# Weight splits on one engine, phase ends reordered by an issue-order constraint, and a recurrence with its state scans between the gate branches

## The chip, the cores and the metric

The kernel runs on one core of one Trainium2 chip, and all work of a forward pass is in this one launch. The metric is device time in microseconds (us) of one execution. Three runs of the kernel before took 1542.88, 1546.4 and 1547.67 us; the median is 1546.4.

A core has five engines that the text names: TensorE (PE in the rows, with its weight loads apart as PEld), VectorE (DVE), ScalarE (ACT), GpSimd (POOL) and SyncE (SP), which here issues every weight transfer. Each engine works through its own queue in order, and engines wait for each other through semaphores.

## The reference, cut to what matters

The input is 256 tokens of width 1024, in fp32, with 256 context tokens. Two blocks follow each other. The first is two layers that mix attention, pooling and a gated linear recurrence; the change leaves most of it alone. The second block is what this text is about:

```
for layer in range(2):
    h = rmsnorm_2(x, norm_mix_pre[layer])
    m = attention_mixer(h, ...) if layer == 0 else recurrent_mixer(h, ...)
    x = x + rmsnorm_2(m, norm_mix_post[layer])
    h = rmsnorm_2(x, norm_ffn_pre[layer])
    f = (silu(h @ w_gate) * (h @ w_up)) @ w_down
    x = x + rmsnorm_2(f, norm_ffn_post[layer])
```

The recurrent mixer, which is the part with changed arithmetic order:

```
gate, xr = split(h @ w_in, 2);  gate = gelu_tanh(gate)
xc = causal depthwise conv of width 4 over xr, + conv_b
r = sigmoid(xc_blocks @ w_a + b_a);  i = sigmoid(xc_blocks @ w_i + b_i)
log_a = -8 * r * softplus(-lam);  a = exp(log_a)
u = sqrt(-expm1(2 * log_a)) * (i * xc)
hs[t] = a[t] * hs[t-1] + u[t]
out = (hs * gate) @ w_out
```

## The kernel before

Every fp32 matmul is made of three products of fp32r halves: each operand is split into a high part (a copy in the narrower type) and a low part (the difference). `mm3` issues high x high, high x low and low x high for each slice of 128 (L395 to L397), called a product below when one such matmul is meant.

A weight tile is 128 x 1024 numbers (512 KB). `W` has SyncE fetch it to a buffer `wr` (L361), ScalarE writes the high part `wh` (L377), and the low part `wl` is a subtraction (L379):

```
        nlo[0] += 1
        S.activation(ch.h, r, AF.Copy)
        eng = G if lopool[0] and nlo[0] % lopool[0] == 0 else V
        eng.tensor_tensor(ch.l, r, ch.h.bitcast(F32), op=OP.subtract)
```

VectorE does the subtraction, but where `lopool` is set every sixth (in `load`) or every third (in the recurrence) goes to GpSimd. `wr`, `wh` and `wl` have three buffers each; `load` fetches a phase's weights ahead, and its tiles 2 to 6 go to five further held buffers (`HW`).

The 256 tokens are two tiles of 128. The phases named below, with their times in the profiled execution: the last projection of the first block (`wout`, 884 to 913 us), the attention's value projection and attention (to 1023), its output projection `ao` (1023 to 1050), the first feed-forward `ffn0` (to 1243), the recurrence (1243 to 1327) with its output projection `ro` (to 1346), and the second feed-forward `ffn1` (1349 to 1533). An output projection (`out_proj`) runs, for each tile, four groups of 24 products (`as2`), one for each 256 columns. A group's result stands in one of three PSUM buffers `mm`. `out_evac` takes it out: ScalarE squares it with a sum (L429) and VectorE multiplies it by a gain (L579). When a tile is done, `residual` scales and adds it (GpSimd's L419 for the inverse root, VectorE's L574, twice 512 columns), and `prenorm` makes the next phase's input: two Squares on ScalarE (L429), L553 on VectorE, L419 on GpSimd, two scalings on VectorE (L557), eight transposes on TensorE (L560), and the split of the transposed tile into `xnah` on ScalarE (L385) and `xnal` on VectorE (L386). Tile 0's chain runs while TensorE does tile 1's products. The next phase's first products need tile 0's `xnah`.

In the recurrence, `conv(i)` is 24 products and three taps on VectorE (L1458); `gates(n)` is 16 products on raw fp32 operands (L1466) for two channel groups, then Tanh, a scaling on VectorE (L1474), Exp and Tanh; `states` is one Sqrt over four channel groups (L1485) with a table load on ScalarE before and after, multiplications on GpSimd (L1487) and scans on VectorE (L1488). `gelu(4)` to `gelu(7)` are 24 products each, a Square (L1493), a VectorE step (L1494), a Tanh (L1495) and a second VectorE step (L1496) that reads the PSUM buffer for the last time. The result is multiplied by the state (L1505) and split for `ro` into `xnbh` on ScalarE (L388) and `xnbl` on VectorE (L389). Where no constraint is written, the order of instructions on an engine is set by a scheduler when the kernel is built, from data dependences, buffers and priorities.

## Time and profile before

| profiled execution | value |
|---|---|
| its own time | 1548.55 us |
| span of the trace | 1546.7 us |
| mean granted TensorE clock | 0.988 of full speed |
| TensorE busy | 1485.1 us, 96% of the span |
| VectorE busy | 955.3 us, 62% |
| ScalarE busy | 757.8 us, 49% |
| GpSimd busy | 248.5 us, 16% |
| weight transfers of 512 KB | 398, median 3.6 us from issue to landing |

The page gives for each engine the time in which it worked; a share of 96% means that TensorE stood still for some 60 us in all. Where those are, and what ended each of them, is read from the waits and the timeline. The granted clock is TensorE's clock as a share of full speed; in the rows below it has two levels, 1.00 (2.4 GHz) and 0.50 (1.2 GHz), and a value between is a mean over a stretch. TensorE works in the order of its queue, and a matmul of 256 columns is shown with 0.28 us though the next starts 0.12 us later, since they are pipelined.

### The profile page before, as it was taken

What the parts mean: (1) busy time and instruction counts of PE and PEld (TensorE: products, weight loads), DVE (VectorE), ACT (ScalarE), POOL (GpSimd) and SP (SyncE); (2) the same over time, 40 slices, a digit from 0 to 9 for tenths busy, and PEclk for the clock granted to TensorE, in tenths of its full rate; (3) what the DMA queues carried; (4) which work ended last, traced back from release to release, by engine and by line L of the source; (5) the groups of instructions that cost most, each with busy time, mean ns of one, the idle gap of its engine ahead of it and who ended that gap; (6) DMA issues with size and microseconds to landing.
All of it is one profiled execution on the core that took longest, in us unless ns stands there. A gap on an engine that the chain in (4) does not pass through costs nothing.

```text
span 1546.7 us, 25517 instructions
## 1 busy us (share of the span) xinstructions
PE 1485.1 (96%) x10206; PEld 1277.8 (83%) x10206; DVE 955.3 (62%) x1530; ACT 757.8 (49%) x1267; POOL 248.5 (16%) x225
## 2 busy tenths in 40 slices
PE   6999999999999999999999989999999997899998
PEld 3766668787877789878989989879999886899986
DVE  5555545866444567766786654866665567756654
ACT  4444344463423356656565454554444458534443
POOL 0101103624200000113442020321000024100000
PEclk8999999999999999999999999999999998899999
DMA  8433322223334465326446563324566654435564
GB/s 341 126 101 131 123 91 82 65 68 95 96 109 151 135 207 160 116 76 207 158 149 193 170 224 124 123 95 157 185 187 185 214 191 148 151 116 186 180 191 134
DMA packets 65639, 229.79 MB, mean 149 GB/s; under 512 B 7280, under 2 KB 7920, under 8 KB 65392
## 3 DMA queue, kind: packets, MB, share of 16 engines
q1 hardware_dynamic: 65520, 228.16, 46.0%
q8 instruction: 80, 1.31, 0.3%
q14 instruction: 39, 0.32, 0.1%
HBM read 227.09 MB, written 1.05 MB: 147 GB/s over the span
## 4 chain that ended last, share of the span: by engine, by line
PE 81%; DVE 6%; DMA 4%; issue 3%; ACT 3%; POOL 2%; SPq 0%; POOLq 0%; DVEq 0%; ACTq 0%
PE mm L395 22%; PE mm L397 22%; PE mm L396 22%; DMA wr<-in_w_dram 3%; PE at L735 2%; DVE wl L379 2%; PE aux L768 2%; ACT wh L377 2%; PE at L755 1%; PE at L859 1%; PE mm L466 1%; POOL wl L379 1%; POOL E L915 1%; POOL qp L895 1%; PE aux L466 0%
## 5 line engine op out<-in xcount | busy, mean ns | idle before, releaser
L379 DVE TENSOR_TENSOR wl<-wr,wh 128x1024 fp32r<-128x1024 f32 x339 | 425.5, 1257 | 340.2 <-ACT wh L377 338.5
L377 ACT ACTIVATE wh<-wr 128x1024 fp32r<-128x1024 f32 x352 | 370.6, 1055 | 426.3 <-PE mm L396 149.7
L395 PE MATMUL mm<-xnah,wh 128*128 128x256 f32 (+1 forms) x1192 | 368.9, 310 | 11.5 <-DVE rt L1496 10.3
L397 PE MATMUL mm<-xnah,wl 128*128 128x256 f32 (+1 forms) x1192 | 363.2, 305 | 4.0 <-DVE wl L379 4.0
L396 PE MATMUL mm<-xnal,wh 128*128 128x256 f32 (+1 forms) x1192 | 361.7, 304 | 0.0
L395 PEld LDWEIGHTS mm<-xnah,wh 128*128 128x128 f32 x1192 | 226.9, 190 | 27.4 <-DVE rt L1496 10.5
L397 PEld LDWEIGHTS mm<-xnah,wl 128*128 128x128 f32 x1192 | 226.8, 190 | 17.3 <-DVE wl L379 5.4
L396 PEld LDWEIGHTS mm<-xnal,wh 128*128 128x128 f32 x1192 | 227.1, 191 | 9.7 <-issue 1.4
L419 POOL TENSOR_TENSOR sm<-sm,minus_half 128x1 f32<-128x1 f32 (+3 forms) x34 | 26.3, 776 | 695.3 <-DVE sm L567 357.6
L397 PE MATMUL mm<-xnbh,wl 128*128 128x512 f32 (+1 forms) x392 | 136.7, 349 | 0.0
L395 PE MATMUL mm<-xnbh,wh 128*128 128x512 f32 (+1 forms) x392 | 135.0, 345 | 0.0
L396 PE MATMUL mm<-xnbl,wh 128*128 128x512 f32 (+1 forms) x392 | 134.8, 344 | 0.0
L395 PE MATMUL mm<-wh,xnah 128*128 128x256 f32 x288 | 83.4, 291 | 6.4 <-ACT xnah L385 6.1
L397 PEld LDWEIGHTS mm<-xnbh,wl 128*128 128x128 f32 x392 | 73.9, 188 | 11.8 <-issue 3.1
L395 PEld LDWEIGHTS mm<-xnbh,wh 128*128 128x128 f32 x392 | 74.0, 189 | 11.2 <-issue 2.9
L397 PE MATMUL mm<-wh,xnal 128*128 128x256 f32 x288 | 82.2, 289 | 0.8 <-DVE xnal L386 0.6
L396 PE MATMUL mm<-wl,xnah 128*128 128x256 f32 x288 | 82.7, 289 | 0.0
L396 PEld LDWEIGHTS mm<-xnbl,wh 128*128 128x128 f32 x392 | 73.9, 188 | 10.1 <-issue 1.2
L396 PE MATMUL mm<-wl,hh 128*128 128x512 f32 x176 | 69.1, 393 | 0.2 <-DVE wl L379 0.2
L397 PE MATMUL mm<-wh,hl 128*128 128x512 f32 x176 | 68.8, 391 | 0.0
L395 PE MATMUL mm<-yh,wh 128*128 128x512 f32 (+1 forms) x192 | 64.9, 338 | 0.0
L396 PE MATMUL mm<-yl,wh 128*128 128x512 f32 (+1 forms) x192 | 64.9, 338 | 0.0
(373 smaller groups left out, 2821.3 us busy)
## 6 DMA issues: line engine op xcount, KB each, us to landing
wr<-in_w_dram SPq DMA_DIRECT2D x398, 512.0 KB, 3.6
wr<-in_w_dram SPq DMA_DIRECT2D x18, 256.0 KB, 3.2
row<-in_rows_dram SPq DMA_DIRECT2D x8, 512.0 KB, 4.9
xt<-in_xin_dram SPq DMA_DIRECT2D x4, 512.0 KB, 5.7
scr<-in_rows_dram SPq DMA_DIRECT2D x8, 256.0 KB, 4.6
xr<-in_xin_dram SPq DMA_DIRECT2D x2, 512.0 KB, 4.6
xc<-in_xin_dram SPq DMA_DIRECT2D x2, 512.0 KB, 5.3
toep<-in_toep_dram SPq DMA_DIRECT2D x1, 1024.0 KB, 7.2
```

The costliest lines, as they stand in the source:

```text
L377: S.activation(ch.h, r, AF.Copy)
L379: eng.tensor_tensor(ch.l, r, ch.h.bitcast(F32), op=OP.subtract)
L395: T.matmul(dst, lh, rh, start=first and i == 0, stop=False)
L396: T.matmul(dst, lh, rl, start=False, stop=False)
L397: T.matmul(dst, ll, rh, start=False, stop=last and i == n - 1)
L419: G.tensor_tensor(y, m, minus_half[:, :n], op=OP.pow)
L466: T.matmul(p[32 * j:32 * j + 32, c0:c0 + 256], sc[:, k * 32:k * 32 + 32], r[:, j, :], start=half == 0, stop=half == 1, tile_position=(0, 3 ...
L735: T.matmul(pa[:, :n], qxs[pr, j][:, c0 + qt * P:c0 + qt * P + P], kxs[pr, j][:, :n], start=True, stop=True)
L755: T.transpose(pa[:, k * 256 + qt * P:k * 256 + qt * P + P], r[qt][:, (2 * k2 + k) * P:(2 * k2 + k + 1) * P], ident)
L768: T.matmul(py[64 * j:64 * j + 64, c0:c0 + 256], v[:, k, h * 64:h * 64 + 64], pTs[j][k // 2][:, k % 2, :], start=k == 0, stop=k == nk - 1, ...
L859: T.matmul(pa[c * s:c * s + s, t * 2 * s:(t + 1) * 2 * s], k_[:, i:i + s], q_[:, :, j:j + s], start=True, stop=True, tile_position=(0, c * s))
L895: (V, G)[j].tensor_tensor(b[r, j, :], gq[r], e[r], op=OP.mult)
```

## The change

First, every weight's low part is computed on VectorE: the choice by `lopool` is gone, and the 13 subtractions that GpSimd did are VectorE's.

Second, `behind(ins)` fixes an issue order within an engine: what is built inside it is queued behind `ins` if both are on the same engine; nothing waits for it on another engine. It is used three times. `load` queues the splits of its third and later weights behind tile 0's last Square on ScalarE and behind tile 0's last scaling (L557) on VectorE, where a `prenorm` of tile 0 came just before. The last group of tile 1 in `out_proj` (columns 768 to 1023) queues its second 12 products behind tile 0's transposes. The last six products (512 columns) of a feed-forward's tile 1 do the same.

Third, in the recurrence: the scaling L1474 is folded into the scale and bias operands of Exp and Tanh, which drops eight VectorE instructions and adds one small one early in the kernel; `states(0, 4)` stands before `gates(3)`; the four products with the gate of channel groups 0 to 3 come before the last gate matmuls' activations, the four remaining gelu branches write into `gl` in place, `states(4, 8)` is written behind the sixth of them, and the four last products with the gate stand at the end. The buffers `t` go from six to four. `gate_half` is defined and not called.

```diff
-    nlo = [0]
     ahead = [0]
-    lopool = [0]
...
         t = pl.tile([P, width], F32, tag="wr", name=nm("wr"), bufs=bufs)
...
         ch.l = tl[:, :nkt * n].rearrange("p (k c) -> p k c", k=nkt)
-        nlo[0] += 1
         S.activation(ch.h, r, AF.Copy)
-        eng = G if lopool[0] and nlo[0] % lopool[0] == 0 else V
-        eng.tensor_tensor(ch.l, r, ch.h.bitcast(F32), op=OP.subtract)
+        V.tensor_tensor(ch.l, r, ch.h.bitcast(F32), op=OP.subtract)
         return ch
...
     def split(o, sl, src, scale=None):
...
-        S.activation(out, src, AF.Square, scale=float(D) ** -0.5, accum_out=acc)
+        return S.activation(out, src, AF.Square, scale=float(D) ** -0.5, accum_out=acc)
...
         t = scratch()
...
         for c in range(2):
-            sq(b[:, c * 512:c * 512 + 512], xt[:, c * 512:c * 512 + 512], ss[:, c:c + 1])
+            q = sq(b[:, c * 512:c * 512 + 512], xt[:, c * 512:c * 512 + 512], ss[:, c:c + 1])
         s1 = sm(1)
...
             sl = slice(k4 * 512, k4 * 512 + 512)
-            V.scalar_tensor_tensor(b[:, sl], xt[:, sl], y, g[:, sl], op0=OP.mult, op1=OP.mult)
+            m = V.scalar_tensor_tensor(b[:, sl], xt[:, sl], y, g[:, sl], op0=OP.mult, op1=OP.mult)
             p = atps()
             for k in range(4):
-                T.transpose(p[:, k * P:(k + 1) * P], b[:, (4 * k4 + k) * P:(4 * k4 + k + 1) * P], ident)
+                tr = T.transpose(p[:, k * P:(k + 1) * P], b[:, (4 * k4 + k) * P:(4 * k4 + k + 1) * P], ident)
             split(xn, (ALL, slice(4 * k4, 4 * k4 + 4), slice(t * P, t * P + P)), p.rearrange("p (k t) -> p k t", k=4))
+        if t == 0:
+            normed[:] = [q, m]
+        return tr
...
     def residual(xt, op, ssp, n):
...
+    normed = [None, None]
     hold = []
...
-        was = lopool[0]
-        lopool[0] = 6
-        r = [HW(k) if 2 <= i < 2 + NHOLD else W(k) for i, k in enumerate(keys)]
-        lopool[0] = was
+        q, m = normed
+        normed[:] = [None, None]
+        r = []
+        for i, k in enumerate(keys):
+            with behind(q if i >= 2 else None), behind(m if i >= 2 else None):
+                r.append(HW(k) if 2 <= i < 2 + NHOLD else W(k))
         return r
...
         chs = load([keyf(cb, hf) for cb in range(4) for hf in range(2)])
+        tr = None
         for i, (tk, xt, gb) in enumerate(tiles):
...
             for cb in range(4):
-                out_evac(as2(chs[2 * cb:2 * cb + 2], a, slice(tk, tk + P)), 256, ops[i], cb * 256, ssp[:, cb:cb + 1], gb)
+                d = as2(chs[2 * cb:2 * cb + 2], a, slice(tk, tk + P), tr if cb == 3 else None)
+                out_evac(d, 256, ops[i], cb * 256, ssp[:, cb:cb + 1], gb)
             with tc.high_priority(offset=600):
                 residual(xt, ops[i], ssp, 4)
-                after(i)
+                tr = after(i)
...
     def trunk_core(l, M, modfill):
-        lopool[0] = 0
         with ExitStack() as st:
...
             pb, m1 = M.poolb(mp), M.merge(1, lambda: M.yp, True)
...
                 drain(fill)
-        lopool[0] = 0
...
     md0, md1, M0, M1 = Obj(), Obj(), Obj(), Obj()
...
     e, s, s2, acc = sm(8), sm(8), sm(8), sm(8)
-    nsp = const.tile([P, 8], F32, name="nsp")
+    nsp = const.tile([P, 16], F32, name="nsp")
     hb = const.tile([P, 16], F32, name="hb")
...
     S.activation(e, e, AF.Exp, scale=-1.0)
...
     V.scalar_tensor_tensor(acc, acc, 2.0, s, op0=OP.mult, op1=OP.add)
-    V.tensor_scalar(nsp, acc, -4.0, None, op0=OP.mult)
+    for i, f in enumerate((-4.0, 4.0)):
+        V.tensor_scalar(nsp[:, 8 * i:8 * i + 8], acc, f, None, op0=OP.mult)
     V.tensor_scalar(hb[:, 0:8], VC("ba"), 0.5, None, op0=OP.mult)
...
     M0.lp = mkpool(left, "l0")
...
                 p = gate(ra, m)
-                t = rp.tile([P, 256], F32, tag="t", name=nm("rt"), bufs=6)
+                t = rp.tile([P, 256], F32, tag="t", name=nm("rt"), bufs=4)
                 S.activation(t, p, AF.Tanh, scale=0.5, bias=hb[:, i:i + 1])
-                V.tensor_scalar(t, t, 1.0, nsp[:, i:i + 1], op0=OP.add, op1=OP.mult)
-                S.activation(av[:, i, :], t, AF.Exp)
-                S.activation(t, t, AF.Tanh, scale=-1.0)
-                t2 = rp.tile([P, 256], F32, tag="t", name=nm("rt"), bufs=6)
+                S.activation(av[:, i, :], t, AF.Exp, scale=nsp[:, i:i + 1], bias=nsp[:, i:i + 1])
+                S.activation(t, t, AF.Tanh, scale=nsp[:, 8 + i:9 + i], bias=nsp[:, 8 + i:9 + i])
+                t2 = rp.tile([P, 256], F32, tag="t", name=nm("rt"), bufs=4)
                 G.tensor_tensor(t2, av[:, i, :], av[:, i, :], op=OP.mult)
...
                 p = gate(ri, m)
...
-        def gelu2(p):
-            t = rp.tile([P, 256], F32, tag="t", name=nm("rt"), bufs=6)
-            S.activation(t, p, AF.Square, scale=float(np.sqrt(0.044715)))
-            V.scalar_tensor_tensor(t, t, 1.0, p, op0=OP.add, op1=OP.mult)
-            S.activation(t, t, AF.Tanh, scale=float(np.sqrt(2 / np.pi)))
-            V.scalar_tensor_tensor(t, t, 1.0, p, op0=OP.add, op1=OP.mult)
-            return t
-        def gelu(i):
-            if i < 2 * NR:
-                t = gl[:, i, :]
-            else:
-                t = gelu2(ws(W(("rg", i)), xn, 0, 256))
+        def gelu2(p, h):
+            S.activation(h, p, AF.Square, scale=float(np.sqrt(0.044715)))
+            V.scalar_tensor_tensor(h, h, 1.0, p, op0=OP.add, op1=OP.mult)
+            S.activation(h, h, AF.Tanh, scale=float(np.sqrt(2 / np.pi)))
+            V.scalar_tensor_tensor(h, h, 1.0, p, op0=OP.add, op1=OP.mult)
+        def out(i):
+            t = gl[:, i, :]
             V.tensor_tensor(t, t, mv[:, i, :], op=OP.mult)
...
-        gl = rp.tile([P, 2 * NR, 256], F32, name="gl")
+        gl = rp.tile([P, 8, 256], F32, name="gl")
         chs = load([("rgt", i, hf) for i in range(NR) for hf in range(2)])
...
             for i in range(NR):
-                late.append((i, t, gelu2(as2(chs[2 * i:2 * i + 2], xn, slice(t * P, t * P + P)))))
+                h = rp.tile([P, 256], F32, tag="t", name=nm("rt"), bufs=4)
+                gelu2(as2(chs[2 * i:2 * i + 2], xn, slice(t * P, t * P + P)), h)
+                late.append((i, t, h))
                 if len(late) > 1:
                     flip(*late.pop(0))
-        lopool[0] = 3
+        def gate_half(i):
+            gelu2(ws(W(("rg", i)), xn, 0, 256), gl[:, i, :])
         for n in range(4):
...
             if late:
...
                 gates(n - 1)
+            if n == 3:
+                states(0, 4)
         gates(3)
-        states(0, 4)
-        states(4, 8)
-        for i in range(8):
-            gelu(i)
-        lopool[0] = 0
+        for i in range(4):
+            out(i)
+        for i in range(4, 8):
+            gelu2(ws(W(("rg", i)), xn, 0, 256), gl[:, i, :])
+            if i == 5:
+                states(4, 8)
+        for i in range(4, 8):
+            out(i)
...
         with ExitStack() as st:
...
                         for j, (k2, ch) in enumerate(held):
-                            part(pd[1], 1, k2, ch, j == R - 1)
+                            with behind(tr if c == 1 and j == R - 1 else None):
+                                part(pd[1], 1, k2, ch, j == R - 1)
                     out_evac(pd[t], 512, ops[t], c * 512, ssp[t][:, c:c + 1], g)
...
                             residual(xr[:, t, :], ops[t], ssp[t], 2)
-                            after(t)
+                            tr = after(t)
         return nxt
...
     xn = attention(xn)
```

What the change does to the queues is shown at three places. Line numbers of the kernel after differ by a few: its L375 is L379 of before, L374 is L377, L381 and L382 are L385 and L386, L431 is L429, L559 is L557, L584 is L579, L574 is L569, L579 is L574, and L1493, L1500 and L1502 are L1485, L1493 and L1495.

VectorE at the end of `wout`, from tile 0's residual on, before (`xs` is tile 0's scaled input, `op` the projection's result, `wl` weight low parts):

```order
L574 SCALAR_TENSOR_TENSOR xr<-op_8537,sm_8702,xr 128x512 x2
L379 TENSOR_TENSOR wl_8902<-wr_8899,wh_8901 128x1024
L379 TENSOR_TENSOR wl_8908<-wr_8905,wh_8907 128x1024
L553 TENSOR_SCALAR sm_8710<-sm_8707 128x1
L569 TENSOR_SCALAR sm_8730<-sm_8730 128x1
L579 TENSOR_TENSOR op_8537<-mm_8731,gx_6628 128x256
L557 SCALAR_TENSOR_TENSOR xs_8706<-xr,sm_8712,row_8535 128x512 x2
L579 TENSOR_TENSOR op_8537<-mm_8759,gx_6628 128x256
L579 TENSOR_TENSOR op_8537<-mm_8787,gx_6628 128x256
```

The same place after:

```order
L579 SCALAR_TENSOR_TENSOR xr<-op_8538,sm_8703,xr 128x512 x2
L375 TENSOR_TENSOR wl_8903<-wr_8900,wh_8902 128x1024
L555 TENSOR_SCALAR sm_8711<-sm_8708 128x1
L559 SCALAR_TENSOR_TENSOR xs_8707<-xr,sm_8713,row_8536 128x512 x2
L375 TENSOR_TENSOR wl_8909<-wr_8906,wh_8908 128x1024
L375 TENSOR_TENSOR wl_8915<-wr_8912,wh_8914 128x1024
L574 TENSOR_SCALAR sm_8731<-sm_8731 128x1
L584 TENSOR_TENSOR op_8538<-mm_8732,gx_6629 128x256
L584 TENSOR_TENSOR op_8538<-mm_8760,gx_6629 128x256
L584 TENSOR_TENSOR op_8538<-mm_8788,gx_6629 128x256
```

Tile 0's scaling L559 moved ahead of two weight splits, and the three evacuations of tile 1's groups (L584) moved behind two further splits; no split stands between them any more.

ScalarE at the end of the recurrence before, from the Squares of `gelu(4)` to `gelu(6)` on (`mm` is the PSUM buffer, `mv` the array of four channel groups, `wh` the high parts of `ro`'s weights):

```order
L1493 ACTIVATE rt_13007<-mm_12982 128x256
L1493 ACTIVATE rt_13046<-mm_13021 128x256
L1493 ACTIVATE rt_13085<-mm_13060 128x256
L377 ACTIVATE wh_13164<-wr_13162 128x1024
L1485 ACT_TABLE_LOAD
L1485 ACTIVATE mv_12360<-mv_12360 128x1024
L1495 ACT_TABLE_LOAD
L1495 ACTIVATE rt_13007<-rt_13007 128x256
L377 ACTIVATE wh_13170<-wr_13168 128x1024
L1495 ACTIVATE rt_13046<-rt_13046 128x256
L1495 ACTIVATE rt_13085<-rt_13085 128x256
```

After, from the Exp of the last gate on:

```order
L1483 ACTIVATE av<-rt_12936,nsp 128x256
L1489 ACTIVATE iv<-at_12943,hb 128x256
L374 ACTIVATE wh_13153<-wr_13151 128x1024
L1484 ACTIVATE rt_12936<-rt_12936,nsp 128x256
L1502 ACTIVATE gl<-gl 128x256
L1500 ACTIVATE gl<-mm_13080 128x256
L374 ACTIVATE wh_13159<-wr_13157 128x1024
L1493 ACT_TABLE_LOAD
L1493 ACTIVATE mv_12361<-mv_12361 128x1024
L374 ACTIVATE wh_13165<-wr_13163 128x1024
L1502 ACT_TABLE_LOAD
L1502 ACTIVATE gl<-gl 128x256
```

The Sqrt with its two table loads now stands between the Square and the Tanh of the last gelu branch alone, and two weight splits stand in that gap; the Tanhs of the three branches before it are ahead of the Sqrt.

ScalarE at the end of `ro` before (`wh` are `ffn1`'s weights, `scr` the Squares of tile 1's groups):

```order
L377 ACTIVATE wh_13506<-wr_13504 128x1024
L429 ACTIVATE scr_13418,sm_13336<-mm_13393 128x256
L377 ACTIVATE wh_13512<-wr_13510 128x1024
L377 ACTIVATE wh_13518<-wr_13516 128x1024
L429 ACTIVATE scr_13446,sm_13336<-mm_13421 128x256
L385 ACTIVATE xnah_13138<-at_13321 128x4x128
L385 ACTIVATE xnah_13138<-at_13329 128x4x128
```

After:

```order
L374 ACTIVATE wh_13495<-wr_13493 128x1024
L431 ACTIVATE scr_13407,sm_13325<-mm_13382 128x256
L374 ACTIVATE wh_13501<-wr_13499 128x1024
L381 ACTIVATE xnah_13127<-at_13310 128x4x128
L381 ACTIVATE xnah_13127<-at_13318 128x4x128
L431 ACTIVATE scr_13435,sm_13325<-mm_13410 128x256
L374 ACTIVATE wh_13507<-wr_13505 128x1024
```

`xnah`, tile 0's transposed input, moved ahead of one weight split and of the last group's Square; on TensorE the transposes that it needs stand 12 products earlier than before.

## Rows read from the trace of the kernel before

**Rows 1.** The page, part 1: each engine's busy time, share of the span, instructions.
```profile
PE 1485.1 (96%) x10206; PEld 1277.8 (83%) x10206; DVE 955.3 (62%) x1530; ACT 757.8 (49%) x1267; POOL 248.5 (16%) x225
```

**Rows 2.** TensorE's waits from 880 us on: total, times, longest.
```profile
PE mm L395 <- DVE rt L1496: 10.3, 1, 10.3
```

**Rows 3.** Line L379, all: shortest, median and longest of one in ns.
```profile
L379 DVE TENSOR_TENSOR wl<-wr,wh x339: 684/1225/2671, 34.8 to 1528.4; 128x1024 fp32r<-128x1024 f32 x169, 128x512 fp32r<-128x512 f32 x1
...
L379 POOL TENSOR_TENSOR wl<-wr,wh x13: 2347/2417/3218, 892.3 to 1351.5; 128x1024 fp32r<-128x1024 f32 x13
```

**Rows 4.** Timeline 1041.5 to 1051 us: start, duration, engine, line.
```profile
1042.11 3.58 DVE L574 SCALAR_TENSOR_TENSOR xr<-op,sm,xr 128x512 f32<-128x512 f32 x2 [0.34 <-POOL sm L419]
...
1042.63 2.50 POOL L379 TENSOR_TENSOR wl<-wr,wh 128x1024 fp32r<-128x1024 f32 x1 [0.56 <-ACT wh L377]
...
1047.61 1.42 DVE L557 SCALAR_TENSOR_TENSOR xs<-xr,sm,row 128x512 f32<-128x512 f32 x2 [0.67 <-POOL sm L419]
```

**Rows 5.** Timeline 891.5 to 895.5 us; in brackets idle time before, and its releaser.
```profile
892.26 2.35 POOL L379 TENSOR_TENSOR wl<-wr,wh 128x1024 fp32r<-128x1024 f32 x1 [31.66 <-ACT wh L377]
...
894.66 0.38 PE L396 MATMUL mm<-wl,moh 128*128 128x256 f32 x1 [2.10 <-POOL wl L379]
```

**Rows 6.** Timeline 1027 to 1030 us.
```profile
1026.30 2.67 DVE L379 TENSOR_TENSOR wl<-wr,wh 128x1024 fp32r<-128x1024 f32 x1 [0.67 <-ACT wh L377]
...
1029.03 0.39 PE L396 MATMUL mm<-wl,xnbh 128*128 128x256 f32 x1 [1.30 <-DVE wl L379]
```

**Rows 7.** Timelines at three phase ends, TensorE's rows that begin after idle time.
```profile
914.59 0.39 PE L395 MATMUL mm<-wh,xnah 128*128 128x256 f32 x1 [1.26 <-ACT xnah L385]
...
1048.42 1.32 PE L560 MATMUL at<-ct,xs 128*128 128x128 f32 x8 [1.21 <-DVE xs L557]
1050.61 0.39 PE L395 MATMUL mm<-wh,xnbh 128*128 128x256 f32 x1 [0.88 <-DVE op L579]
...
1243.19 0.39 PE L395 MATMUL mm<-wh,xnah 128*128 128x256 f32 x1 [0.84 <-ACT xnah L385]
...
1244.57 0.38 PE L397 MATMUL mm<-wh,xnal 128*128 128x256 f32 x1 [0.64 <-DVE xnal L386]
```

**Rows 8.** Timeline 1300 to 1331 us, ScalarE and TensorE.
```profile
1307.37 0.91 ACT L1493 ACTIVATE rt<-mm 128x256 f32<-128x256 f32 x3
...
1309.66 1.28 ACT L1485 ACT_TABLE_LOAD   x1
...
1312.03 1.28 ACT L1495 ACT_TABLE_LOAD   x1
...
1314.25 0.58 PE L395 MATMUL mm<-xnah,wh 128*128 128x256 f32 x1 [10.30 <-DVE rt L1496]
```

**Rows 9.** Groups of instructions, 1243 to 1330 us: busy, mean ns, idle before.
```profile
L1487 POOL TENSOR_TENSOR iv<-iv,mv 128x256 f32<-128x256 f32 x8 | 7.0, 904 | 0.4 <-ACT mv L1485 0.4
...
L1488 DVE TENSOR_TENSOR_SCAN mv<-av,iv 128x256 f32<-128x256 f32 x8 | 5.5, 698 | 0.0
...
L1474 DVE TENSOR_SCALAR rt<-rt,nsp 128x256 f32<-128x256 f32 x8 | 4.0, 504 | 0.0
```

**Rows 10.** Stretches: length, busy time (instructions) per engine, PEclk, DMA share, GB/s.
```profile
1060.00:1100.00 40.00, 40.00 (x340) 40.00 (x339) 21.51 (x33) 16.16 (x26) 0.95 (x2) 1.00 0.46 149
...
1314.25:1323.79 9.54, 9.54 (x58) 9.33 (x58) 9.07 (x15) 5.31 (x10) 0.62 (x1) 0.72 0.48 155
...
1350.35:1353.76 3.41, 3.31 (x16) 3.29 (x16) 3.41 (x4) 1.76 (x4) 2.29 (x1) 0.50 0.91 308
```

**Rows 11.** Timeline 1335 to 1352 us.
```profile
1337.40 2.41 POOL L379 TENSOR_TENSOR wl<-wr,wh 128x1024 fp32r<-128x1024 f32 x1 [2.85 <-ACT wh L377]
...
1339.75 1.54 POOL L419 TENSOR_TENSOR sm<-sm,minus_half 128x1 f32<-128x1 f32 x1
...
1347.11 1.06 ACT L377 ACTIVATE wh<-wr 128x1024 fp32r<-128x1024 f32 x1 [2.56 <-DMA wr<-in_w_dram]
...
1349.06 0.39 PE L395 MATMUL mm<-wh,xnah 128*128 128x256 f32 x1 [3.46 <-ACT xnah L385]
```

12 lines of the change are left out of this document (8 added, 4 removed).

## The prediction

> **What bounds the kernel now.** I read the page's busy times first: TensorE works 96% of the span, the next engine, VectorE, 62% [rows 1]. So a change outside TensorE can only give back part of the 61.6 us in which TensorE stands still, or time that it works at the lower clock. The first 880 us have no line of this change on TensorE's path: its queue is the same there, and none of GpSimd's 13 subtractions lies before 892.3 us [rows 3]. Next I read TensorE's waits from 880 us on. One wait stands out, 10.3 us for the last step of a gelu branch (L1496) [rows 2]; the others are of 0.6 to 3.5 us at the starts and ends of phases, and I read each in the timeline with what its releaser had been doing [rows 4 to 8, 11]. Last I read TensorE's granted clock by stretches [rows 10].
>
> **Price of a product.** In an undisturbed stretch 340 matmuls take 40.00 us [rows 10]: 0.118 us each, 24 of them 2.83 us.
>
> **The splits.** A subtraction takes 1.22 us on VectorE and 2.42 on GpSimd (medians) [rows 3]. 13 moved ones add 13 x 1.22 = 15.9 us to VectorE and take 31 us from GpSimd. There is a second price: while GpSimd's subtraction runs, VectorE's own operations stretch. Two L574 took 3.58 us under a GpSimd split of 2.50 us, where two L557 of the same size took 1.42 a little later [rows 4]; a VectorE split took 2.67 us in place of 1.22 [rows 6].
> - Start of `wout`: TensorE waits 2.10 us for a GpSimd split that began at 892.26 [rows 5]. On VectorE, whose next split there is one weight later, it would begin as early and end at 893.48, not 894.61. Gain 1.1 to 1.2; I take 1.2, since the first product follows at once.
> - Start of `ao`: the stretched split ends at 1028.97 and TensorE goes on at 1029.03 after 1.30 us [rows 6]. Unstretched it ends by 1027.55; with the moved split ahead of or behind it the wait goes, but part returns one weight later. Gain 1.0 of 1.30.
> - End of `ffn0`: waits of 0.84 and 0.64 us for `xnah` and `xnal` [rows 7], with a residual in tile 0's chain that lies under a GpSimd split as in [rows 4]. By that pair (3.58 and 1.42) the chain gets 2.2 us earlier and its transposes stand six products of 512 columns earlier. I leave 0.35 for the low part. Gain 1.1.
>
> **The issue order at the ends of `out_proj`.** Tile 0's scaling goes ahead of weight splits, and evacuations of tile 1 go behind them. What waits behind: the evacuation frees a PSUM buffer, and tile 1's fourth group needs one.
> - End of `wout`: 1.26 us for `xnah` goes [rows 7]. But the first evacuation now stands behind two scalings (1.42 [rows 4]) and two splits (2.44): TensorE has three groups, and I work out a wait of 1.1 us for the buffer. Gain 0.2; if VectorE gets through in time 1.26, if a split also waits for its transfer -1.
> - End of `ao`: 1.21 and 0.88 us [rows 7]; the same new wait remains, 1.4 or so. Gain 0.6, bounds -1 and 2.1.
> - End of `ro`: 3.46 us [rows 11]. `xnah` stood on ScalarE behind a split that had waited 2.56 us for its transfer, until 1347.11; the chain itself was late through GpSimd's split at 1337.40, behind which the inverse root of one number took 1.54 us [rows 11]. After, `xnah` stands ahead of that split, the transposes 12 products (1.4 us) earlier, and that GpSimd split is gone. Tile 1's last product ends near 1345.6, `xnah` about then, and TensorE would begin at 1345.8 and not 1349.06. Gain 3.2; bounds 1.6 (if the low part `xnal`, behind a split of 1.22 us, holds the third kind of product) and 3.4.
>
> **The recurrence.** Before, three gelu branches hold all three PSUM buffers while ScalarE does the second Sqrt with its two table loads; TensorE waits 10.30 us until 1314.25 [rows 8]. Then 58 matmuls take 9.54 us at a mean granted clock of 0.72 [rows 10], where 58 x 0.118 = 6.8 would do: 2.7 lost to the lower clock. Together 13.0. After, I find three waits.
> 1. `gates(3)` now needs the last convolution's last tap, and on VectorE 15 operations of 256 columns lie from its first to its last, among them the four products with the gate and their low parts. One takes between 0.36, half of a 512-column scaling [rows 4], and 0.504, L1474's mean [rows 9]; at an estimate of 0.42 that is 6.3 us, at the upper end 7.6; TensorE has 24 products (2.83) and about 1 us of `gates(2)` meanwhile. I take 2.4, bounds 0 and 4.
> 2. Only the last gelu branch stands around the Sqrt. Its buffer is free after its Square (0.30: three took 0.91), a weight split 1.06 [rows 11], load 1.28, Sqrt with its start 1.09 (1310.94 to 1312.03), a split 1.06, load 1.28, and 0.94 from the load's end to TensorE [rows 8]: 7.0. TensorE has two half groups, 24 products, 2.83. Wait 4.2.
> 3. Then `ro` needs the last four channel groups' low parts. VectorE does a product (0.4), three scans (3 x 0.70 [rows 9]), two splits (2.44), two products (0.8) and a low part (0.4): 6.1 us. TensorE has 18 products for it, 2.1: wait 4.0, and 0.6 more for the groups that follow. 4.6, bounds 2 and 6.
>
> Sum 11.2, so 1.8 less than 13.0, with the clock back at its upper level. The eight L1474 (4.0 us [rows 9]) go from VectorE and from between two ScalarE steps; they lie under TensorE's work and I count nothing. If the last gate's chain is what the Sqrt waits for, it is 0.5 more. Four `t` buffers where there were six cost nothing, since gelu results now stand in `gl`.
>
> **Clock.** At 1350.35 to 1353.76 the granted clock is 0.50 [rows 10], right behind the 3.46 us wait. Half of 3.41 us, 1.7, is lost. Without that wait I expect it to stay up, but the new waits could bring another such stretch: 1.0.
>
> **Sum.** 1.2 + 1.0 + 1.1 + 0.2 + 0.6 + 3.2 + 1.8 + 1.0 = 10.1 us. Against the profiled execution's own time 1548.55 - 10.1 = 1538.4. That execution is 2.15 us above the median of the runs, 1546.4, so I forecast 1536.3.
>
> **The rivals.**
> *The recurrence gives nothing, chance 0.26.* GpSimd keeps its multiplications there. L1487 takes 0.90 us in the mean [rows 9], and VectorE's splits become denser around them by five. If each of the last four waits for one split, that is 4 x 1.22 = 4.9 us on the chain to the scans; at half of it, 2.4, the 1.8 are gone: gain 7.7, time 1538.7. With the whole 4.9, or if the three waits still pull the clock down (2.7), the gain is about 5, and 1541.3. For it: the row pair in [rows 4], where the later of the two stretches. Against it: L1487 stands on an idle GpSimd, and only three splits lie between those scans.
> The Trainium skill, "SBUF — State Buffer", section "Who interferes with whom", has VectorE with two SBUF inputs and GpSimd on an exclusive lock: the second to issue is blocked for the whole of the other. The trace agrees (1.42 against 3.58 us under a split of 2.50). By that rule more splits on VectorE block GpSimd's multiplications for up to the whole 1.22 us, which is this rival's upper price.
>
> *The ends do only half of what they are for, chance 0.13.* An issue order does not make data earlier. If weight transfers, 91% of the queues' time at 1350 us [rows 10], or `xnal` are late, `ro` gives 1.6 and `ffn0` 0.5: gain 7.9, time 1538.5.
>
> *More than forecast, chance 0.11.* No wait at `gates(3)`, 2.3 us for the low parts, and the clock up throughout: 2.4 + 2.3 + 0.7 more, 15.5 in all, 1530.9.
>
> *Slower, chance 0.04.* VectorE becomes the bound at the four phase ends. Each end has six splits (7.3 us), residual and scalings (2 x 1.42), four evacuations (1.6) and two `xnal` (1.4): 13.1 us in the 11.3 us of four groups. If the 1.8 us fall on TensorE at all four ends and take the place of the gains there, and only the recurrence's 1.8 stay: +7.2 - 1.8 = 5.4, 1551.8. It decides from 2.5 us at each end if the other gains stand. Against it: the splits of the fourth pair are needed only 8.5 us after the phase begins, and VectorE works 21.5 of 40 us there [rows 10].
>
> The Trainium skill, "ScalarE: Activation LUTs", section "What ACT_TABLE_LOAD costs", adds to a load of 1.283 us a drain of 1.38, which would make the second wait 7.0 where I have 4.2, and the time 1539.1. The trace shows the load alone: 1.28, and the next begins 1.09 us after it with a whole Sqrt between [rows 8]. I count this case in the first rival's chance, with 0.02 of it.
>
> **How the numbers follow.** The forecast has 0.46. Faster by over 0.3% (4.6 us, about what this measurement can tell; below 1541.8): the forecast, the ends by half, more than forecast and 0.15 of the first rival's 0.26, 0.85. Within 0.3%: the other 0.11. Slower 0.04. The range goes from the best case less some of the runs' own scatter, 1530.5, to the first rival's worst end with a wait of an evacuation more, 1542.5; I leave 0.08 below and 0.1 above.
>
> **What the profile after would show.** No split on GpSimd, and no VectorE scaling of 512 columns near 2.9 us. No wait of 2.10 near 892. At the end of `wout` a wait for an evacuation (L579), not for `xnah`. In the recurrence no wait over 5 us, but three: for a tap (L1458), for the last gelu step (L1496) and for a low part (L389), and a granted clock near 1.00. `ffn1` begins without idle time over 0.6 us. The prediction is wrong if the recurrence's waits still add up to 13, if TensorE waits for weight splits (L379) by more than 2 us at a phase end, or if the clock falls behind the new waits.

## The result, and the profile after

The kernel after took 1537.68 us (median of four runs, 1536.97 to 1537.92), the kernel before 1545.52 beside it: ratio 0.9949, interval 0.9932 to 0.9967, so 5 to 10 us faster. The forecast was 1536.3 with 1530.5 to 1542.5. Seven more runs of the same kernel, in a later series, gave 1536.67 and a ratio of 0.9955 (0.9936 to 0.9973). The profiled execution took 1536.97 us, its span is 1535.0 us.

The page of the kernel after, part 1, answers to [rows 1]:

```profile
PE 1482.4 (97%) x10206; PEld 1277.9 (83%) x10206; DVE 957.0 (62%) x1536; ACT 761.6 (50%) x1267; POOL 213.8 (14%) x212
```

TensorE's busy time is 2.7 us less (the same products in less time), and its idle time fell from 61.6 to 52.6 us. GpSimd lost 35 us of work. TensorE's waits from 880 us on, total, times and longest (L584 is before's L579, L1503 its L1496, L382 and L385 its L386 and L389):

```profile
PE mm L391 <- DVE gl L1503: 5.0, 2, 4.7
PE at L1475 <- ACT xnbh L384: 4.2, 1, 4.2
PE mm L391 <- DVE op L584: 3.9, 3, 1.6
...
PE mm L393 <- DVE xnbl L385: 1.8, 1, 1.8
...
PE mm L393 <- DVE xnal L382: 0.9, 2, 0.6
```

The kernel before had, beside the 10.3 us of [rows 2]:

```profile
PE mm L395 <- ACT xnah L385: 6.1, 4, 3.5
...
PE mm L395 <- DVE op L579: 1.9, 3, 0.9
```

The wait of 10.3 us is gone, and of the 6.1 us for `xnah` 0.3 is left. In their place stand two waits of some 4.5 us in the recurrence, 1.8 us for a low part, and 3.9 us for evacuations. No wait for a GpSimd split is left. The residual scaling shows the stretching gone, as one line's instructions with shortest, median and longest in ns, before and after:

```profile
L574 DVE SCALAR_TENSOR_TENSOR xr<-op,sm,xr x20: 740/751/2908, 904.1 to 1543.0; 128x512 f32<-128x512 f32 x20
...
L579 DVE SCALAR_TENSOR_TENSOR xr<-op,sm,xr x20: 743/748/753, 900.9 to 1531.3; 128x512 f32<-128x512 f32 x20
```

After, all 20 take 0.75 us; before, the longest took 2.91, one of the two that took 3.58 together under a GpSimd split [rows 4]. Four places in the timeline after: the last group of `wout` and of `ao` behind tile 0's transposes, and the first product of the value projection and of `ffn1`:

```profile
908.40 0.39 PE L391 MATMUL mm<-wh,moh 128*128 128x256 f32 x1 [1.56 <-DVE op L584]
...
911.39 0.28 PE L391 MATMUL mm<-wh,xnah 128*128 128x256 f32 x1
...
1043.73 0.39 PE L391 MATMUL mm<-wh,xnbh 128*128 128x256 f32 x1 [1.52 <-DVE op L584]
...
1341.20 0.28 PE L391 MATMUL mm<-wh,xnah 128*128 128x256 f32 x1
```

Both profiles hold the same number of matmuls, so the same product can be found in each and its start compared:

| first product of | before, us | after, us | earlier by |
|---|---|---|---|
| `wout` | 881.80 | 881.24 | 0.6 |
| the value projection | 914.59 | 911.39 | 3.2 |
| `ao` (its main run) | 1023.40 | 1018.26 | 5.1 |
| `ffn0` | 1053.59 | 1046.70 | 6.9 |
| the recurrence | 1243.19 | 1235.56 | 7.6 |
| `ffn1` | 1349.06 | 1341.20 | 7.9 |
| end of the span | 1546.7 | 1535.0 | 11.7 |

These are two single executions, and 11.7 us is 3.9 more than the medians differ by. Between the recurrence and `ffn1`, where 5.0 us were forecast, the profile shows 0.2: what `ro`'s end gave, the recurrence took. The last 3.8 us come after: the half-level stretch behind the 3.46 us [rows 10], 1.7, and a faster rate of products (last section). The first product of `ffn1` has no idle time ahead of it where before had 3.46. Here is the recurrence after, TensorE's rows that begin after a wait:

```profile
1291.20 2.90 PE L1475 MATMUL at<-xconv,wr 128*128 128x256 f32 x6 [4.25 <-ACT xnbh L384]
...
1314.15 0.58 PE L391 MATMUL mm<-wh,xnbh 128*128 128x256 f32 x1 [4.73 <-DVE gl L1503]
...
1319.72 0.38 PE L393 MATMUL mm<-wh,xnbl 128*128 128x256 f32 x1 [1.83 <-DVE xnbl L385]
...
1325.91 0.38 PE L391 MATMUL mm<-wh,xnbh 128*128 128x256 f32 x1 [0.85 <-DVE op L584]
```

4.25 us before the last gates, 4.73 for the last gelu branch's buffer, 1.83 for a low part, 0.85 for an evacuation: with 0.30 elsewhere 12.0 us. And the clock fell three times; these are the parts of the half-level stretches in which TensorE worked (length, busy time by engine, then PEclk):

```profile
1291.20:1296.71 5.51, 5.51 (x20) 4.97 (x21) 4.24 (x10) 1.37 (x3) 0.00 (x0) 0.50 0.14 32
...
1314.15:1317.19 3.04, 3.04 (x14) 3.04 (x15) 3.04 (x5) 0.94 (x2) 0.21 (x1) 0.50 0.56 175
1320.61:1324.02 3.41, 3.41 (x18) 3.41 (x17) 0.40 (x2) 0.00 (x0) 0.00 (x0) 0.50 0.35 138
```

5.51 + 3.04 + 3.41 = 11.96 us at 0.50: up to 6.0 us lost, where the kernel before lost 2.7 behind its one wait [rows 10]. The stretches are not the same in every execution: the second profile of after has 6.8 and 10.2 us at 0.50 there, around the same waits.

### The profile page after: what moved, and what is told of

It reads as the page before. It is cut to its first block, busy times and chain, and to the rows that moved or that the text cites. A ratio compares the mean times of both kernels' runs of the same rounds, so it can differ in the third digit from the quotient of the medians.

```text
span 1535.0 us, 25518 instructions
## 1 busy us (share of the span) xinstructions
PE 1482.4 (97%) x10206; PEld 1277.9 (83%) x10206; DVE 957.0 (62%) x1536; ACT 761.6 (50%) x1267; POOL 213.8 (14%) x212
## 4 chain that ended last, share of the span: by engine, by line
PE 83%; DVE 6%; DMA 3%; ACT 3%; issue 3%; POOL 1%; SPq 0%; DVEq 0%; POOLq 0%; ACTq 0%
PE mm L391 23%; PE mm L393 23%; PE mm L392 23%; DMA wr<-in_w_dram 3%; PE at L745 2%; DVE wl L375 2%; PE aux L778 2%; PE at L765 1%; ACT wh L374 1%; PE at L869 1%; PE mm L468 1%; PE at L1475 1%; PE aux L468 1%; PE at L951 0%; PE aux L1373 0%
## 5 line engine op out<-in xcount | busy, mean ns | idle before, releaser
L375 DVE TENSOR_TENSOR wl<-wr,wh 128x1024 fp32r<-128x1024 f32 x352 | 439.2, 1250 | 340.4 <-ACT wh L374 337.5
L374 ACT ACTIVATE wh<-wr 128x1024 fp32r<-128x1024 f32 x352 | 370.9, 1056 | 429.6 <-PE mm L392 155.6
```

Of the source, the lines that this page charges most:

```text
L375: V.tensor_tensor(ch.l, r, ch.h.bitcast(F32), op=OP.subtract)
```

## The experiments

Each ratio is to runs of the kernel before in the same series; the medians of before were 1545.74 (first four experiments), 1544.53 (next four), 1545.07 (next three) and 1545.17 us. One kernel's runs scatter by 1 to 9 us, so an interval is some 4 to 6 us wide, and the profile has to say where a difference lies. Each run has one profile, and these scatter too: the first product of `wout` begins between 878 and 885 us, though the changes under test lie behind it. So stages are compared from there on.

**Splits and order with the recurrence of before** (`e1`): everything between `gates` and the last `gelu` as it was.

```diff
-                S.activation(av[:, i, :], t, AF.Exp, scale=nsp[:, i:i + 1], bias=nsp[:, i:i + 1])
+                V.tensor_scalar(t, t, 1.0, nsp[:, i:i + 1], op0=OP.add, op1=OP.mult)
+                S.activation(av[:, i, :], t, AF.Exp)
...
+        states(0, 4)
+        states(4, 8)
-        for i in range(4, 8):
-            out(i)
+        for i in range(8):
+            gelu(i)
```

> The kernel after with the recurrence of before (its instructions, its order, its buffers); splits on VectorE and the issue order stay. Theory: the new recurrence costs time. In the profile after, TensorE's waits in it (4.25, 0.30, 4.73, 1.83, 0.85 us) and three stretches at half clock (2.7, 1.5 and 1.7 us lost) make 17.9 us where before had 14.5. Then this kernel is about 3.4 us faster than after: 1534.3, and its recurrence shows one wait near 10 us and one half-clock stretch. Rival: the new recurrence gains the forecast 1.8 us and the profile after is one bad execution; then this is 1539.5.

1541.42 us, ratio 0.9972 (0.9958 to 0.9987): 4.3 us faster than before, and by the ratios some 3 us slower than after, with intervals that overlap. That the new recurrence costs time is not so; the theory fell. Its waits (total, times, longest):

```profile
PE mm L391 <- DVE rt L1504: 13.7, 1, 13.7
```

The old recurrence's wait has grown from 10.3 to 13.7 us: VectorE now does the splits that GpSimd did there. So the new recurrence, with its 12.0 us and three half-level stretches, stands against 13.7 us with one and a further wait of 1.3 before the last gates. The two profiles' spans are 1537.8 and 1535.0 us, and that is no more than the slower rate of products explains (335 matmuls in the 40 us from 1100, 336 from 1400, where after has 339). From the recurrence's first product to that of `ffn1` this profile takes 105.2 us, after 105.6: it shows no gain of the new recurrence over the old one.

**The recurrence alone** (`e2`): the diff's third part on the kernel before; with it GpSimd keeps its third of the splits.

```diff
-        for i in range(8):
-            gelu(i)
...
+        for i in range(4, 8):
+            gelu2(ws(W(("rg", i)), xn, 0, 256), gl[:, i, :])
+            if i == 5:
+                states(4, 8)
+        for i in range(4, 8):
+            out(i)
```

> The kernel before with the new recurrence alone; every sixth and third split stays on GpSimd, no issue order. Theory: about 3.4 us slower than before (1549), two waits of 4 to 5 us in the recurrence in place of one of 10.3, and the clock down two or three times. Rival: 1.8 us faster than before (1543.7).

1543.32 us, ratio 0.9988 (0.9975 to 1.0002): 2.4 us by the medians, an interval that just holds zero. The rival stands nearer. Waits:

```profile
PE mm L395 <- DVE gl L1495: 5.7, 2, 3.6
PE mm L395 <- ACT xnah L385: 5.7, 4, 3.7
...
PE at L1467 <- ACT av L1475: 3.1, 1, 3.1
```

5.7 and 3.1 us in place of 10.3, and the wait for `xnah` much as before (6.1).

**The splits alone** (`e3`):

```diff
-        eng = G if lopool[0] and nlo[0] % lopool[0] == 0 else V
-        eng.tensor_tensor(ch.l, r, ch.h.bitcast(F32), op=OP.subtract)
+        V.tensor_tensor(ch.l, r, ch.h.bitcast(F32), op=OP.subtract)
```

> The kernel before with all splits on VectorE and nothing else. Theory: the starts of wout and ao and the end of ffn0 give their 3 us, the end of ro half of its 3.2 (the GpSimd split is gone, the queue order on ScalarE is as before): 4 to 5 us faster than before, 1541. No VectorE operation of 512 columns over 1.5 us under a split. Rival: the issue order is what carries the gain; then this is within 1.5 us of before.

1546.87 us, ratio 1.0004 (0.999 to 1.0018): nothing gained; the rival is right. The waits name the reasons:

```profile
PE mm L394 <- DVE rt L1495: 13.8, 1, 13.8
PE mm L394 <- ACT xnah L384: 8.0, 5, 2.9
```

13.8 us in the recurrence, and 8.0 us for `xnah` where before had 6.1. At the ends of `ao` and `ro` `xnah` stands on ScalarE behind a weight split that had waited for its transfer, 1.01 and 2.26 us; at `ro`:

```profile
1351.84 1.06 ACT L377 ACTIVATE wh<-wr 128x1024 fp32r<-128x1024 f32 x1 [2.26 <-DMA wr<-in_w_dram]
1352.81 1.07 ACT L384 ACTIVATE xnah<-at 128x512 fp32r<-128x512 f32 x2
```

**The order alone** (`e4`): `behind` in `load`, `out_proj` and the feed-forward, with GpSimd's splits kept.

```diff
+            with behind(q if i >= 2 else None), behind(m if i >= 2 else None):
+                r.append(HW(k) if 2 <= i < 2 + NHOLD else W(k))
...
+                d = as2(chs[2 * cb:2 * cb + 2], a, slice(tk, tk + P), tr if cb == 3 else None)
```

> The kernel before with the issue order behind tile 0's transposes, Squares and scalings alone; GpSimd keeps its splits, and the recurrence is that of before. Theory: it takes away part of the 3.46 us wait at the end of ro and the half-clock stretch behind it, and brings the wait for an evacuation at the other ends: 2 to 4 us faster than before, 1542. Rival: without VectorE's splits the stretched operations still delay tile 0's chain and it gives nothing, 1545.

1545.46 us, ratio 0.9998 (0.9984 to 1.0012). Again the rival. Waits:

```profile
PE mm L395 <- DVE rt L1511: 10.4, 1, 10.4
PE mm L395 <- DVE op L588: 5.1, 3, 2.4
```

The wait for `xnah` is gone from the list's head, but 5.1 us for evacuations came in its place (1.9 before): they stand behind VectorE operations that GpSimd's splits still stretch, a residual scaling at `ao` (3.56 us for two of 512 columns) and at `wout` a weight split, which ran beside a GpSimd split of 2.84 us:

```profile
906.18 3.38 DVE L379 TENSOR_TENSOR wl<-wr,wh 128x1024 fp32r<-128x1024 f32 x1
```

By the medians the three parts alone come to +1.1, -0.3 and -2.4 us, together -1.6; splits and order together give -4.3, the whole -7.9. Where this lies, in us from a stage's first product to that of the next one, in each profile:

| profile | `wout` to `ao` | `ffn0` | recurrence and `ro` | `ffn1` to the end |
|---|---|---|---|---|
| before | 171.8 | 189.6 | 105.9 | 197.7 |
| splits (`e3`) | 168.8 | 193.4 | 109.0 | 196.2 |
| order (`e4`) | 171.1 | 191.3 | 103.1 | 194.7 |
| recurrence (`e2`) | 171.3 | 190.2 | 106.6 | 196.9 |
| splits and order (`e1`) | 165.6 | 190.0 | 105.2 | 195.3 |
| after | 165.5 | 188.9 | 105.6 | 193.8 |
| after again (`e5`) | 165.0 | 188.3 | 105.3 | 194.1 |

From `wout` to `ao` splits and order need each other: 3.0 and 0.7 us alone, 6.2 together; all eight profiles that have both take 165.0 to 166.9. The order takes away what the splits cost at the phase ends, and the splits take away the stretching that spoils the order. What the new recurrence adds to these two isn't shown: its own stage is no shorter (105.6 and 105.3 against 105.2), and what the whole has over them lies in the two feed-forwards, where the products come faster (last section). The new recurrence was not run with only one of the other two parts.

**The kernel after again** (`e5`), unchanged.

> The kernel after, unchanged, beside the others. The single parts gave 1.1 us slower (splits), 0.3 faster (order) and 2.4 faster (recurrence), together 1.6 faster, where the whole gave 7.8. Theory: the parts work only together, so the whole stays near 1537.7, 8 us faster than before. Rival: the four runs of it were low by chance, and the whole is near the sum of the parts and of splits with order (4.3): 1541 to 1542.

1536.67 us, ratio 0.9955 (0.9936 to 0.9973): the theory. The profile shows much the same waits in the recurrence (4.25, 4.73, 1.36 us), and the clock at half level around them.

**GpSimd's third split back in the recurrence** (`e6`):

```diff
-        V.tensor_tensor(ch.l, r, ch.h.bitcast(F32), op=OP.subtract)
+        eng = G if lopool[0] and nlo[0] % lopool[0] == 0 else V
+        eng.tensor_tensor(ch.l, r, ch.h.bitcast(F32), op=OP.subtract)
...
+        lopool[0] = 3
         for n in range(4):
```

> The kernel after, with every third split inside the recurrence back on GpSimd. Theory: the splits moved to VectorE cost there (the profile of splits alone loses 4 to 5 us between the last of ffn0 and ro, that of order alone nothing), so this is 2 to 3 us faster than after, with the wait before the last gates shorter than 4.25. Rival: the new recurrence has absorbed them, and GpSimd's split stretches VectorE's operations as before: 0 to 1 us slower than after.

1536.27 us, ratio 0.9946 (0.9928 to 0.9963): no difference from after. The waits of the recurrence only shift:

```profile
PE mm L395 <- DVE gl L1507: 5.2, 2, 2.7
PE at L1479 <- ACT av L1487: 3.1, 1, 3.1
```

3.1 us before the last gates where after has 4.2, 5.2 in two for the gelu buffers where it has 5.0.

**No order in `load`** (`e7`):

```diff
-            with behind(q if i >= 2 else None), behind(m if i >= 2 else None):
-                r.append(HW(k) if 2 <= i < 2 + NHOLD else W(k))
+            r.append(HW(k) if 2 <= i < 2 + NHOLD else W(k))
```

> The kernel after without the order behind tile 0's Square and scaling in load; the last half group behind the transposes stays. Theory: the order in load is what makes VectorE's added splits harmless at the phase ends (splits alone gained nothing), so without it 3 to 4 us of the gain go: 1541. Rival: the transposes' place in TensorE's queue carries it, and this is within 1 us of after.

1539.68 us, ratio 0.9968 (0.9953 to 0.9983): 3 us slower than after by the medians, with intervals that overlap. The waits at the phase ends:

```profile
PE mm L393 <- DVE xnal L382: 2.7, 5, 0.6
PE mm L391 <- DVE op L584: 2.2, 3, 0.9
```

2.7 us for `xnal` (0.9 after) and 2.2 for evacuations (3.9 after): the same sum, so the phase ends don't show 3 us. At `ro`'s end `xnah` is not late here either: 0.3 us for it and 0.65 for `xnal`. Whether the order in `load` is worth those 3 us stays open.

**The transposes last again** (`e9`):

```diff
-                d = as2(chs[2 * cb:2 * cb + 2], a, slice(tk, tk + P), tr if cb == 3 else None)
+                d = as2(chs[2 * cb:2 * cb + 2], a, slice(tk, tk + P))
...
-                            with behind(tr if c == 1 and j == R - 1 else None):
-                                part(pd[1], 1, k2, ch, j == R - 1)
+                            part(pd[1], 1, k2, ch, j == R - 1)
```

> The kernel after without the order behind tile 0's transposes (the last 12 products of a projection's tile 1 and the last six of the feed-forward stand ahead of them again); the order in load stays. Theory: tile 0's transposes come 1.4 us later and TensorE waits for xnah at the ends of the projections, 0.7 to 1.4 us each: 2 to 3 us slower than after, 1539.5. Rival: the wait for an evacuation was at those ends anyway and only changes its name, and ro's end has slack: within 1 us of after.

1540.17 us by the median, but ratio 0.9958 (0.9941 to 0.9974), that of after. The row for evacuations is that of after (3.9, 3, 1.6), and one more decides:

```profile
PE mm L391 <- ACT xnah L381: 1.0, 3, 0.4
```

The waits for `xnah` are 1.0 us in all, 0.4 at most, where the theory had 0.7 to 1.4 each, and none of them is at `ro`. With the order in `load` in place, the 12 products behind the transposes are not needed to remove the 3.46 us; the rival is nearer.

**The scaling back on VectorE** (`e10`):

```diff
+                V.tensor_scalar(t, t, 1.0, nsp[:, i:i + 1], op0=OP.add, op1=OP.mult)
-                S.activation(av[:, i, :], t, AF.Exp, scale=nsp[:, i:i + 1], bias=nsp[:, i:i + 1])
-                S.activation(t, t, AF.Tanh, scale=nsp[:, 8 + i:9 + i], bias=nsp[:, 8 + i:9 + i])
+                S.activation(av[:, i, :], t, AF.Exp)
+                S.activation(t, t, AF.Tanh, scale=-1.0)
```

> The kernel after with the eight scalings of the gates back on VectorE and Exp and Tanh without operands of scale and bias. Theory: VectorE's queue is what the last gates wait for in the recurrence, and four of the eight (0.35 each) stand in it ahead of the last tap: 1 to 2 us slower than after. Rival (the prediction's): they lie under TensorE's work, within 0.5 us.

1536.73 us, ratio 0.9943 (0.9927 to 0.996): no difference, as the prediction had it. The scheduler found another order with it, with 1.2 us before the last gates and a wait of 4.4 for `xnbh`.

**The taps first** (`e8`): what the last gates wait for is VectorE's queue. After's VectorE there:

```profile
1281.71 1.69 DVE L375 TENSOR_TENSOR wl<-wr,wh 128x1024 fp32r<-128x1024 f32 x1
...
1286.35 1.57 DVE L375 TENSOR_TENSOR wl<-wr,wh 128x1024 fp32r<-128x1024 f32 x1
...
1290.62 0.86 DVE L1467 SCALAR_TENSOR_TENSOR xconv<-mm,vt,xconv 128x255 f32<-128x255 f32 x2
...
1293.08 0.47 DVE L1467 SCALAR_TENSOR_TENSOR xconv<-mm,vt,xconv 128x255 f32<-128x255 f32 x1
```

The taps of the last two convolutions (L1467, three for each channel group) stand between splits (L375), scans and products with the gate (L1508). TensorE goes on at 1291.20, just after the last tap of the seventh group (the first of the pair at 1290.62); the last tap of the eighth ends at 1293.55. The row names ScalarE's `xnbh` as the releaser; that the taps decide is shown by this run. It queues the scans and products of channel groups 0 to 3 behind the last tap, and the last two gelu branches behind the second Sqrt on ScalarE:

```diff
+        with behind(tap):
+            states(0, 4)
         gates(3)
-        for i in range(4):
-            out(i)
+        with behind(tap):
+            for i in range(4):
+                out(i)
...
+        root = states(4, 8)
+        for i in range(6, 8):
+            p = ws(W(("rg", i)), xn, 0, 256)
+            with behind(root):
+                gelu2(p, gl[:, i, :])
```

> The kernel after with another order in the recurrence: scans and products of channel groups 0 to 3 queue on VectorE behind the last convolution's last tap, and the last two gelu branches on ScalarE behind the second Sqrt. Theory: the 4.25 us wait before the last gates is a queue of VectorE and goes, with the half-clock stretch behind it (2.7); one wait near 5 us at the Sqrt stays: 2 to 5 us faster than after, 1533 to 1536. Rival: the wait only moves to the Sqrt and ro's low parts, the clock falls there, and it is within 1 us of after.

1530.17 us, ratio 0.9907 (0.9889 to 0.9925): 6.5 us faster than after in the same series, more than expected. The last tap begins at 1285.38, the wait before the last gates is gone, and the recurrence's waits are 5.5 and 1.6 us. From the recurrence's first product to that of `ffn1` the profile takes 98.4 us, after 105.6: the gain lies there. The two orders were not run apart.

```profile
1285.38 0.47 DVE L1467 SCALAR_TENSOR_TENSOR xconv<-mm,vt,xconv 128x255 f32<-128x255 f32 x1
```

```profile
PE mm L391 <- ACT xnbh L384: 5.5, 1, 5.5
PE mm L391 <- DVE gl L1506: 1.6, 2, 0.8
```

The clock still falls once, in the 5.47 us wait; the part of that stretch with work in it:

```profile
1306.06:1309.83 3.77, 3.77 (x16) 3.48 (x17) 3.77 (x9) 2.62 (x4) 0.00 (x0) 0.50 0.39 135
```

**The taps first, the wait filled** (`e11`):

```diff
+                if fill[0] and i == 0 and cb == 1:
+                    pf = auxps()[:, :256]
+                    with behind(half0[0]):
+                        for _ in range(fill[0]):
+                            z = T.matmul(pf, a.h[:, 0, 0:P], chs[0].h[:, 0, :], start=True, stop=True)
```

> The kernel with the taps first (1530.2), and 40 products more on TensorE whose results nobody reads, behind ro's first 12 products, where it waits 5.47 us: the work of 4.7 us lies in that wait. Theory: the clock falls because TensorE stands still there; busy, it keeps the granted clock at 1.00 where taps first has 0.50 for 6.8 us, in which it works 3.7 us: about 1.9 us faster than taps first, 1528.3. Rival: the clock falls all the same or later, and it is as fast or 0.5 us slower.

1529.35 us, ratio 0.9894 (0.9879 to 0.991). The added products (L624) and what begins behind them:

```profile
1301.10 4.43 PE L624 MATMUL aux<-wh,xnbh 128*128 128x256 f32 x36
1306.78 0.39 PE L391 MATMUL mm<-wh,xnbh 128*128 128x256 f32 x1 [1.25 <-ACT xnbh L384]
...
1310.55 0.51 PE L393 MATMUL mm<-wh,xnbl 128*128 128x256 f32 x2 [1.03 <-DVE xnbl L385]
```

```profile
1296.00:1315.00 19.00, 15.23 (x121) 14.40 (x120) 17.19 (x27) 14.86 (x22) 5.08 (x5) 1.00 0.55 168
```

The granted clock is 1.00 throughout, where the kernel without them has 0.50 for 6.8 us: half of the theory. But TensorE waits again, 1.25 and 1.03 us, for high and low parts that ScalarE and VectorE make; the other half, 1.9 us, is not shown (0.8 us between medians, overlapping intervals, and 98.4 us from the recurrence's first product to that of `ffn1` in both profiles).

**The kernel after, the wait before the last gates filled** (`e12`): 34 such products ahead of `gates(3)`.

```diff
+            with behind(last_mm[0]):
+                for _ in range(34):
+                    z = T.matmul(pf, ch.h[:, 0, 0:P], xn.h[:, 0, 0:256], start=True, stop=True)
```

> The kernel after with 34 products more on TensorE whose results nobody reads, ahead of the last gates, where it waits 4.25 us: 4.0 us of work in that wait. Theory: the granted clock stays at 1.00 where the profile after has 0.50 from 1289.88 to 1296.71, and the last gates and 17 products that took 5.51 us end 2.75 us sooner; the chain to ro hangs on them, so 2 to 2.7 us faster than after (1534.5). Rival, as filling the later wait showed: the clock stays up, but the time is set by VectorE and ScalarE, which don't run at TensorE's clock, and the next wait grows by what is saved: within 1 us of after (1536.7).

1537.99 us, runs from 1531.35 to 1539.27, ratio 0.9939 (0.9918 to 0.996): the time doesn't tell it from after. The rows of this stretch:

```profile
1290.15 4.19 PE L1554 MATMUL aux<-xnah,wh 128*128 128x256 f32 x34
...
1309.44 0.56 PE L393 MATMUL mm<-wh,xnbh 128*128 128x256 f32 x1 [2.49 <-DVE gl L1509]
...
1315.89 0.39 PE L393 MATMUL mm<-wh,xnbh 128*128 128x256 f32 x1 [3.55 <-DVE gl L1509]
...
1320.00 0.39 PE L393 MATMUL mm<-wh,xnbh 128*128 128x256 f32 x1 [0.64 <-DVE gl L1509]
```

```profile
1290.00:1300.00 10.00, 9.79 (x72) 9.20 (x71) 9.22 (x21) 5.80 (x14) 1.69 (x3) 1.00 0.16 52
```

The clock stays at 1.00, and the later waits are 2.49 + 3.55 + 0.64 = 6.7 us, against 0.30 + 4.73 + 1.83 = 6.9 after: the later waits did not grow. From the recurrence's first product to that of `ffn1` the profile takes 102.9 us, after 105.6 and 105.3; but the runs without the order in `load` and without the transposes' order, which have the same recurrence, take 106.4 and 103.8, so one profile doesn't show that the gain is kept. In the whole time it can't be seen.

## Why the prediction came out

The time was right (1536.3 forecast, 1537.7 measured), the terms less so, and that they add up is luck. In the profile `wout` to `ao` gave 6.3 us where 3.0 were forecast, the recurrence and `ro` 0.2 where 5.0 were, and what follows `ro` 3.8 where 1.0 was.

- **GpSimd's splits: mechanism right, one cost left out.** No residual scaling is stretched any more, and the wait of 2.10 at 892 is gone. But the 15.9 us that came to VectorE were put under TensorE's work at no cost. Splits alone show it: 3.5 us more in the old recurrence's wait, 1.9 more for `xnah`, and no gain in time. The gain at `wout` was under-sized in turn: 2.6 us from its first product to that of the value projection, against 1.4 forecast, since a wait of 0.95 us for a weight's high part just ahead shrank to 0.16 along with the 2.10; and 1.9 more from there to `ao`, where the kernel before had its clock at half level behind its waits at `wout`'s end, which the sum didn't count:

```profile
916.85:920.27 3.42, 3.42 (x19) 3.42 (x18) 3.42 (x5) 2.28 (x5) 2.17 (x2) 0.50 0.71 218
```

- **The ends of `wout` and `ao`: right.** A new wait of 1.1 and 1.4 us for an evacuation was forecast; 1.56 and 1.52 came. (In the order shown for `wout`, the scaling moved ahead of one weight split; the other still stands in front of it.)
- **The end of `ffn0`: right**, with 0.64 for the low part where 0.35 was left.
- **The end of `ro`: right in size.** 3.2 was forecast, all of 3.46 went, and with it the half-level stretch behind it (1.0 forecast, 1.7 there). Of the reasons given, neither order is needed by itself: without the early transposes no wait for `xnah` or `xnal` is left at `ro`, without the order in `load` 0.3 us for `xnah` and 0.65 for `xnal`. Splits with neither, and the old recurrence, kept 2.9 us of it; order with GpSimd's splits left 0.7 and 0.6.
- **The recurrence: the step that failed is "with the clock back at its upper level".** The three waits were forecast as 2.4, 4.2 and 4.6, 11.2 in all; they were 4.25, 5.03 and 2.68, 12.0. The last gates waited for taps behind the queue that was named, but longer, because two splits of 1.6 us were in it. The clock fell at each of the three, 6.0 us lost at most, where the sum had none here and 0.7 under its clock term; a clock that falls behind the new waits is one of the prediction's own signs of being wrong. So the recurrence and `ro` together gave 0.2 us in the profile and not 5.0. Filling the first of these waits with work kept the clock up (`e12`), as did filling the wait that taps first leaves (`e11`): it falls there because TensorE stands still. The waits of 1.56 and 1.52 us at the ends of `wout` and `ao` brought no such stretch.
- **The eight scalings: right**, nothing.
- **The first rival** (the recurrence gives nothing) came true in the profile. Of its two reasons, GpSimd's multiplications are the smaller: the eight take 8.3 us where before had 7.0 [rows 9], 1.3 of the 4.9 that it priced, and with GpSimd's third split back the time is the same. The other, that the three waits still pull the clock down, is what the profile shows. The total stayed because `wout`, the value projection and a faster rate of products (below) gave what the recurrence did not.

The Trainium skill's page "ScalarE: Activation LUTs", section "What ACT_TABLE_LOAD costs", adds a drain of 1.38 us to a table load. The wait for the last gelu buffer, which had two loads in it, came out at 4.73 us where 4.2 was forecast without a drain and 7.0 with two, and the Sqrt begins 0.01 us after the first load's end, the second load right behind the split that follows: the trace shows no drain.

```profile
1307.78 1.28 ACT L1493 ACT_TABLE_LOAD   x1
1309.07 1.06 ACT L1493 ACTIVATE mv<-mv 128x1024 f32<-128x1024 f32 x1
```

## What to carry to other kernels

Parts of a change that each gain nothing can gain together: here splits and order each took away the other's cost, and only together were they faster. A total that comes out as forecast doesn't show that its terms do: compare the same product's start in both profiles, stage by stage. A wait should be priced with the clock behind it: read the granted clock right after it. And when an engine off the bound decides a wait, look at what stands ahead of the awaited instruction in its queue; an order that put the awaited taps first, and the last gelu branches behind the root, gave 6.5 us, nearly as much as the whole change.
